# Later sums for the convolution's norm in a two-layer hybrid block on one Trainium2 core

## The chip, the cores and the metric

The kernel runs on one core of one Trainium2 chip, alone. The metric is the device time of one execution in microseconds: 1804.47 us, the median of three executions from 1803.35 to 1806.31 us. All arithmetic on the matrix engine (PE) takes float32 data that the kernel has split into a high and a low part, so each weight block is multiplied three times (high by high, high by low, low by high).

## The reference, cut to what matters

The model has two layers. In each, a normalised input `h` is projected and goes through three branches (sparse attention, retention, convolution). Each branch's output is projected to 1024 channels, multiplied by a sigmoid gate of its own, and the three are summed; then come an output projection and a feed-forward part.

```python
h = _rmsnorm(x, norm_mix[l]); z = h @ w_in[l]
...
y = lax.conv_general_dilated(u, kern, ...)        # 31 taps for each of 512 channels
y = _layernorm(y + dw_b, ln_g, ln_b)              # over the 512 channels of a token
o_conv = jax.nn.silu(y)
br = jnp.stack([o_nsa, o_ret, o_conv], axis=2)
proj = jnp.einsum('bsnc,ncd->bsnd', br, w_branch[l])
gate = jax.nn.sigmoid(m_g).reshape(B, S, N_BRANCH, D_MODEL)
merged = jnp.sum(gate * proj, axis=2)
x = x + merged @ w_out[l]
```

The norm of the convolution is the part that moves. It needs two sums over channels for each token (for the mean, and for the variance of what is left), and the second needs the first.

## The kernel before

**Layout.** Activations lie with channels on the 128 partitions and the 512 tokens along the row, so a sum over channels is made on PE: `column_sums` multiplies four blocks of 128 tokens by a column of ones, and `rows_to_bcast` spreads a value per token over all partitions by four transposes.

**Convolution.** 124 taps (31 for each of four blocks of channels) are multiply-add instructions on the vector engine (DVE, line 338). They are dropped one or two at a time behind other DVE work. What is left when attention starts, `late_taps`, is spread over the attention's 64 inner steps: a tap's place is found from the step's number over `T_SLOTS` (52), so the last tap stands behind step 51 of 0 to 63.

**Attention** runs as 16 units, numbered u = 4j + k here: j is one of four pairs of heads, k counts two groups by two kinds of attention. A unit makes scores (PE, from line 707 on, tile `sc`), adds a bias and finds the row's extreme (DVE, line 712), takes the exponential (ScalarE, ACT, line 714), scales (line 719), transposes (PE, line 722), splits the result (ACT line 727, DVE line 728), and multiplies it with the values (PE, tile `av`). Line 739 ends a pair's group with `on`. The score tile `S` has three buffers and `sc` two banks.

**Fillers.** The gates and the retention branch's products do not depend on attention. They stand in the list `pending`: 8 products `mix(1, RO, m)`, then 16 gates `gate_ahead` for the other two branches. A gate is 24 matmuls with 512 columns into one bank `mm`, then one DVE and one ACT instruction, and a store to DRAM. Its weight block is loaded by SP, copied by ACT (line 145) and split by GpSimd (POOL, line 148) ahead of it. One entry runs before attention; 19 are handed out after units 0 to 15 by `more` (one each, two after units 5, 10 and 15); the last four, `HELD`, come when attention has been traced. The PE instructions of the entries of unit u stand behind that unit's first score matmul (`issue_after(marks[u].ins)`).

**Banks.** All gates, products, `query` projections and also the norm's sums use the three PSUM banks of tag `mm`, which are given out in the order in which the program asks for them.

**Order.** A planner that simulates the kernel writes out a fixed order for each engine. It takes the ready instruction that comes first in the program; what the program asks for later may go first only while earlier work is not ready.

**The norm** is a generator, `conv_norm` (line 585), of four steps: three additions on DVE (588 to 590); mean sums on PE, spread, four subtractions (597), squares, additions (601); the sums of squares and the root (POOL, line 206); and last `rows_to_bcast`, then for each of four blocks a multiplication (608), a scaling (609), a tanh (611), a product (612), a copy and a subtraction (112, 113), which give the convolution's output `OC`. From unit 12 on, when no tap is left, `more` takes one step per unit, ahead of that unit's fillers: additions at unit 12, mean at 13, squares at 14, the last step at 15.

**After attention** come the splits of its output into `OS`, eight products `mix(0, OS, m)` (12 matmuls each), eight `mix(2, OC, m)` and the output projection. A mix loads its stored gate `g`, and DVE joins it with the product (464) and adds it to `merged` (468).

Of the kernel before, what the change touches and what calls it, by code (L numbers as in the profile page):

```python
# [66 lines left out]
def block_kernel(ctx: ExitStack, tc: tile.TileContext, a, out):  # L67
# [7 lines left out]

    T_ROT, T_SCORE, T_KEYS, T_SLOTS = 1, 2, 3, 52


    AHEAD, F_KEYS, HELD = 16, 1, 4

    def tl(pool, tag, bufs, shape=(P, T), dtype=F):
        count[0] += 1
        return pool.tile(list(shape), dtype, name=f"{tag}_{count[0]}", tag=tag, bufs=bufs)
# [7 lines left out]
    def small(shape, dtype=F):  # L93
        if math.prod(shape[1:]) <= 8:
            return tl(base, "n", 40, shape, dtype)
        return tl(base, "m", 7, shape, dtype)
# [3 lines left out]
    def ps(tag, shape=(P, T)):  # L100
        return tl(psum, tag, PS_BUFS[tag], shape)
# [51 lines left out]
    def wblock(src, nk=KC, n=P):  # L153

        return wsplit(raw(lambda t: [(t, src)], nk, n), nk, n)

    def proj(o, w, x, nk=KC):

        h, l = w
        for k in range(nk):  # L160
            xh, xl = x[k]
            mm(o, h[:, k, :], xh, k == 0, False)
            mm(o, h[:, k, :], xl, False, False)
            last = mm(o, l[:, k, :], xh, False, k == nk - 1)
        return last
# [104 lines left out]
    for l in range(DEPTH):  # L270
# [56 lines left out]
        todo = [(c, k) for c in range(4) for k in range(CW)]  # L327

        def conv_taps(n):

            while n and todo and todo[0][0] < len(us):
                c, k = todo.pop(0)
                n -= 1
                w, x = ccol[:, c, l * CW + k:l * CW + k + 1], us[c][:, k:k + T]
                if k == 0:
                    nc.vector.tensor_scalar(yc[c], x, w, par(20 + c), op0=OP.mult, op1=OP.add)
                else:
                    nc.vector.scalar_tensor_tensor(yc[c], x, w, yc[c], op0=OP.mult, op1=OP.add)  # L338
# [49 lines left out]
        for h in range(4):  # L388
            if h % 2 == 0:
# [3 lines left out]
                for i in range(NB):  # L393
# [3 lines left out]
                    m = small((P, 2))  # L397
# [17 lines left out]
            for j in range(NB):  # L415
                n = T - j * P
# [27 lines left out]
        def gate(n, m):  # L444
            pg = ps("mm")
            proj(pg, wblock(w_f[FB_MG + n * KC + m]), X)
            t = tl(base, "g", 3)
            nc.vector.tensor_mul(t, pg, rs)
            nc.scalar.activation(t, t, AF.Tanh, scale=0.5)
            return t  # L450
# [5 lines left out]
        def mix(n, o, m):  # L456
            if (n, m) in gated:
                t = tl(base, "g", 3)
                dma(t, gdram[n * KC + m])
            else:  # L460
                t = gate(n, m)
            po = ps("mm")
            proj(po, wblock(a["w_b"][l, n, m], 4), o, 4)
            nc.vector.scalar_tensor_tensor(t, t, 1.0, po, op0=OP.add, op1=OP.mult)
            if n == 1:
                dma(mdram[m], t)
            else:
                nc.vector.tensor_add(merged[m], merged[m], t)

        pending = [lambda m=m: mix(1, RO, m) for m in range(KC)]  # L470
# [3 lines left out]
        def fill(n):  # L474
            for _ in range(min(n, len(pending))):
                pending.pop(0)()
# [108 lines left out]
        def conv_norm():  # L585

            s, s2 = ut(), ut()
            nc.vector.tensor_add(s, yc[0], yc[1])
            nc.vector.tensor_add(s2, yc[2], yc[3])
            nc.vector.tensor_add(s, s, s2)  # L590
            yield
            mean = small((P, NB))
            nc.vector.tensor_scalar(mean, column_sums(s, tag="mm"), 1.0 / 512, None, op0=OP.mult)
            pm = rows_to_bcast(mean, "mm")
            acc = None
            for c in range(4):
                nc.vector.tensor_sub(yc[c], yc[c], pm)
                s = ut()
                nc.scalar.activation(s, yc[c], AF.Square)
                if acc is not None:  # L600
                    nc.vector.tensor_add(s, s, acc)
                acc = s
            yield
            rstd = rsqrt_rows(column_sums(acc, tag="mm"), 1.0 / 512)
            yield
            pr = rows_to_bcast(rstd, "mm")
            for c in range(4):
                nc.vector.tensor_mul(yc[c], yc[c], pr)
                nc.vector.tensor_scalar(yc[c], yc[c], par(24 + c), par(28 + c), op0=OP.mult, op1=OP.add)
                y = ut()  # L610
                nc.scalar.activation(y, yc[c], AF.Tanh, scale=0.5)
                nc.vector.scalar_tensor_tensor(y, y, 1.0, yc[c], op0=OP.add, op1=OP.mult)
                h, lo = tl(cp, "yc", 4, dtype=FR), ut(FR) if c < 3 else tmp(dtype=FR)
                split(h, lo, y)
                OC.append((h, lo))

        normed = conv_norm()
# [25 lines left out]
        def query(j):  # L643
            w = wblock(w_f[FB_Q + j])
            pq = ps("mm")
            proj(pq, w, X)
            tq = tl(ap, "tq", 2)
            nc.vector.scalar_tensor_tensor(tq, pq, -0.125, rs, op0=OP.mult, op1=OP.mult)
            return tq

        def attention_pair(j, tq, more):
            QS, bias = [], []
            for g in range(2):
# [41 lines left out]
            for g in range(2):  # L695
# [4 lines left out]
                for br in range(2):  # L700
# [30 lines left out]
                    for k, c0 in enumerate((0, 512, 896, 1152)):  # L731
                        n = T - k * P
                        lhs = V[k][:, 2 * br + g, :]
                        mm(av[:, k * P:], lhs, ph[:, c0:c0 + n], False, False)
                        mm(av[:, k * P:], lhs, pl[:, c0:c0 + n], False, br == 1 and k == NB - 1)
                    more(j, 2 * g + br)
                t = tmp()
                nc.scalar.activation(t[nat], av[oth], AF.Copy)
# [3 lines left out]
        ON, marks, tqs = [], [], [query(0)]  # L742
        late_taps = len(todo)

        def more(j, k):

            if k == 0 and j + 1 < HPG:
                tqs.append(query(j + 1))
            if not todo:
                next(normed, None)  # L750
            u = 4 * j + k
            with tc.issue_after(marks[u].ins):
                fill(paced * (u + 1) // 16 - paced * u // 16)

        for j in range(HPG):
            ON.append(attention_pair(j, tqs[j], more))
        conv_taps(len(todo))
        for _ in normed:
            pass
        with tc.issue_after(marks[-1].ins):  # L760
            fill(len(pending))

        phase.close()
        phase = ExitStack()
# [6 lines left out]
        for m in range(KC):  # L771
            merged[m] = tl(pp, "mg", 8)
            dma(merged[m], mdram[m])
            mix(0, OS, m)
        for m in range(KC):
            mix(2, OC, m)

# [110 lines left out]
```

## Time and profile before

| | |
|---|---|
| median of 3 executions | 1804.47 us |
| the profiled execution | 1804.74 us |
| its span | 1803.0 us |
| PE busy | 1757.3 us (97%) |
| DVE busy | 1104.4 us (61%) |
| ACT busy | 774.9 us (43%) |
| POOL busy | 500.6 us (28%) |

The times in the rows below count from the start of the span of this execution. A row of a timeline has start, duration, engine, line, operation, output and inputs, shape and count; what stands in brackets is the engine's idle time before it and what ended it. Matmuls overlap, so the distance of two starts is the price of what lies between, not the duration.

### The profile page before, as it was taken

How to read it: one execution, taken by the hardware profiler on the slowest of the kernel's cores; microseconds unless marked ns; L12 is line 12 of the kernel's file. 1: busy time of each engine (PE TensorE's matmuls, PEld its weight loads, DVE VectorE, ACT ScalarE, POOL GpSimd, SP SyncE). 2: the span in 40 equal slices, each digit the busy share in tenths (PEclk: the TensorE clock that was granted, in tenths of full speed). 3: DMA queues.
4: the chain of work that ended last, by engine and by line, in shares of the span. 5: the costliest groups of instructions: out<-in, count | busy, mean ns of one | idle time of the engine just before them, and what ended most of it. 6: DMA issues, size and time to landing. Idle time of an engine off the chain costs nothing.

```text
span 1803.0 us, 23260 instructions
## 1 busy us (share of the span) xinstructions
PE 1757.3 (97%) x8592; PEld 1473.8 (82%) x8592; DVE 1104.4 (61%) x1979; ACT 774.9 (43%) x1421; POOL 500.6 (28%) x420
## 2 busy tenths in 40 slices
PE   8899899989999999999999999999899999999997
PEld 7788788868888888888898888888688888888886
DVE  6976978887554344434459778878857443434344
ACT  4433466766343232323434344667553341323241
POOL 4454444323471000000255543343137500000000
PEclk9999999989999999999999999999899999999998
DMA  4222623221753323333422232332147323332321
GB/s 167 87 88 61 203 94 122 96 71 65 233 169 96 101 96 93 95 96 102 135 94 89 87 127 83 98 131 90 41 161 227 119 94 94 93 94 94 105 85 68
DMA packets 70802, 195.82 MB, mean 109 GB/s; under 512 B 8945, under 2 KB 9329, under 8 KB 70689
## 3 DMA queue, kind: packets, MB, share of 16 engines
q1 hardware_dynamic: 70688, 194.34, 33.6%
q8 instruction: 68, 1.11, 0.3%
q14 instruction: 46, 0.37, 0.1%
HBM read 177.51 MB, written 19.42 MB: 109 GB/s over the span
## 4 chain that ended last, share of the span: by engine, by line
PE 67%; issue 20%; DVE 10%; ACT 2%; DMA 1%; SPq 0%; POOLq 0%; POOL 0%; DVEq 0%; ACTq 0%
PE mm L109 58%; PE sc L109 3%; DVE yc L338 3%; PE av L109 3%; PE tp L722 2%; PE tp L109 1%; DVE XP L500 1%; DVE kv L563 1%; DVE qk L386 1%; ACT s L719 0%; DVE pt L728 0%; ACT wh L145 0%; DVE rr L364 0%; PE tp L190 0%; DVE s L712 0%
## 5 line engine op out<-in xcount | busy, mean ns | idle before, releaser
L109 PE MATMUL mm<-X,wh 128*128 128x512 f32 x2432 | 777.4, 396 | 12.2 <-ACT X L214 6.1
L148 POOL TENSOR_TENSOR wl<-wr,wh 128x512 fp32r<-128x512 f32 (+2 forms) x344 | 436.2, 1290 | 563.2 <-ACT wh L145 540.6
L145 ACT ACTIVATE wh<-wr 128x1024 fp32r<-128x1024 f32 (+2 forms) x301 | 296.9, 987 | 681.9 <-PE mm L109 554.5
L109 PEld LDWEIGHTS mm<-X,wh 128*128 128x128 f32 x2432 | 455.3, 189 | 103.1 <-ACT X L214 6.3
L109 PE MATMUL mm<-X,wl 128*128 128x512 f32 x1216 | 479.5, 394 | 0.4 <-DVE wl L150 0.4
L109 PEld LDWEIGHTS mm<-X,wl 128*128 128x128 f32 x1216 | 230.2, 189 | 46.5 <-DVE wl L150 0.9
L338 DVE SCALAR_TENSOR_TENSOR yc<-u,ccol,yc 128x512 f32<-128x512 f32 x240 | 214.2, 894 | 1.7
L150 DVE TENSOR_TENSOR wl<-wr,wh 128x1024 fp32r<-128x1024 f32 x129 | 158.1, 1225 | 38.4 <-ACT wh L145 38.4
L109 PE MATMUL mm<-fa,wh 128*128 128x512 f32 x512 | 160.2, 395 | 0.0
L109 PE MATMUL mm<-bo,wh 128*128 128x512 f32 x512 | 160.0, 391 | 0.0
L805 DVE SCALAR_TENSOR_TENSOR t<-mm,rs 128x512 f32<-128x512 f32 x64 | 43.9, 691 | 161.5 <-PE mm L109 155.9
L227 POOL TENSOR_TENSOR t<-t,t 128x512 f32<-128x512 f32 x18 | 27.4, 1523 | 333.7 <-DVE wl L150 310.7
L206 POOL TENSOR_TENSOR n<-n,mhalf 128x4 f32<-128x4 f32 x15 | 16.5, 1101 | 372.3 <-DVE n L204 372.3
L109 PE MATMUL mm<-kv,wh 128*128 128x512 f32 x384 | 119.5, 389 | 0.0
L109 PEld LDWEIGHTS mm<-fa,wh 128*128 128x128 f32 x512 | 96.1, 188 | 23.2
L109 PEld LDWEIGHTS mm<-bo,wh 128*128 128x128 f32 x512 | 96.0, 188 | 19.7
L109 PE MATMUL mm<-fa,wl 128*128 128x512 f32 x256 | 100.5, 395 | 0.0
L109 PE MATMUL mm<-bo,wl 128*128 128x512 f32 x256 | 100.2, 392 | 0.0
L714 ACT ACTIVATE s<-s,n 128x128 f32<-128x128 f32 (+3 forms) x128 | 71.4, 559 | 46.9 <-DVE n L712 46.3
L109 PE MATMUL mm<-wh,X 128*128 128x256 f32 (+1 forms) x480 | 90.1, 286 | 0.0
L728 DVE TENSOR_TENSOR pt<-tp,pt 128x128 fp32r<-128x128 f32 (+1 forms) x192 | 70.0, 372 | 32.7 <-ACT pt L727 32.4
L816 DVE TENSOR_TENSOR yc<-yc,mm 128x512 f32<-128x512 f32 x32 | 22.0, 687 | 105.6 <-PE mm L109 105.6
(219 smaller groups left out, 2463.9 us busy)
## 6 DMA issues: line engine op xcount, KB each, us to landing
wr<-in_w_dram SPq DMA_DIRECT2D x128, 512.0 KB, 3.5
wr<-in_w_f_dram SPq DMA_DIRECT2D x87, 512.0 KB, 3.3
wr<-in_w_b_dram SPq DMA_DIRECT2D x48, 256.0 KB, 2.7
wr<-in_w_t_dram SPq DMA_DIRECT2D x16, 512.0 KB, 3.4
gd<-g SPq DMA_DIRECT2D x32, 256.0 KB, 2.0
g<-gd SPq DMA_DIRECT2D x32, 256.0 KB, 2.8
wr<-in_w_o_dram SPq DMA_DIRECT2D x16, 512.0 KB, 3.6
md<-g SPq DMA_DIRECT2D x16, 256.0 KB, 2.9
```

The costliest lines, as they stand in the source:

```text
L109: return nc.tensor.matmul(o, l, r, start=start, stop=stop)
L145: nc.scalar.activation(h, t, AF.Copy)
L148: nc.gpsimd.tensor_sub(l[:, k], t[:, k], f(h[:, k]))
L150: nc.vector.tensor_sub(l, t, f(h))
L227: (nc.vector if c == KC - 1 or first_time else nc.gpsimd).tensor_add(s, s, acc)
L338: nc.vector.scalar_tensor_tensor(yc[c], x, w, yc[c], op0=OP.mult, op1=OP.add)
L386: nc.vector.tensor_sub(QLr[h][half], pt[nat], f(QHr[h][nat]))
L714: nc.scalar.activation(s, s, AF.Exp, scale=-1.0, bias=mx[:, i:i + 1], accum_out=den[:, i:i + 1])
L722: nc.tensor.transpose(pt[:, k * P:(k + 1) * P], cols[i][:, k * P:(k + 1) * P], ident)
L728: low = nc.vector.tensor_sub(vl, src, f(vh))
L805: nc.vector.scalar_tensor_tensor(t, pf, 0.0, rs, op0=OP.max, op1=OP.mult)
L816: nc.vector.tensor_add(xT[m], xT[m], pf)
```

## The change

The taps are spread over 56 steps in place of 52. No step of the norm is taken inside attention. When attention has been traced, the first step (additions) is taken and two held gates follow; the second step (mean, subtractions, squares), and the other two held gates; the third (sums of squares, root), and no gate. The last step comes in the loop of the first products, after `mix(0, OS, 1)`.

```diff
-    T_ROT, T_SCORE, T_KEYS, T_SLOTS = 1, 2, 3, 52
+    T_ROT, T_SCORE, T_KEYS, T_SLOTS = 1, 2, 3, 56
...
             if k == 0 and j + 1 < HPG:
                 tqs.append(query(j + 1))
-            if not todo:
-                next(normed, None)
             u = 4 * j + k
...
         conv_taps(len(todo))
-        for _ in normed:
-            pass
-        with tc.issue_after(marks[-1].ins):
-            fill(len(pending))
+
+        for n in (HELD // 2, HELD - HELD // 2, 0):
+            next(normed)
+            with tc.issue_after(marks[-1].ins):
+                fill(n)
...
             mix(0, OS, m)
+            if m == 1:
+                next(normed, None)
```

## Rows read from the trace of the kernel before

**Rows 1.** Page, part 2: PE busy and granted clock in 40 slices
```profile
PE   8899899989999999999999999999899999999997
PEclk9999999989999999999999999999899999999998
```

**Rows 2.** Windows: stretch, length, busy time and instructions by engine, PE clock, DMA
```profile
core 0: us, PE busy (x) PEld busy (x) DVE busy (x) ACT busy (x) POOL busy (x), PEclk, DMA share, GB/s
...
380.85:412.30 31.45, 24.43 (x112) 18.23 (x111) 27.36 (x78) 19.41 (x56) 2.64 (x2) 0.78 0.08 28
412.30:465.10 52.80, 52.80 (x261) 44.42 (x260) 32.50 (x67) 31.98 (x66) 17.37 (x15) 1.00 0.37 120
465.10:487.60 22.50, 22.50 (x98) 18.13 (x97) 13.23 (x15) 5.71 (x10) 13.72 (x16) 1.00 0.73 245
487.60:510.00 22.40, 22.40 (x99) 18.28 (x98) 17.54 (x22) 9.49 (x14) 16.43 (x15) 1.00 0.71 214
1264.45:1296.10 31.65, 24.90 (x111) 18.76 (x110) 27.29 (x75) 19.15 (x55) 2.63 (x2) 0.73 0.07 25
1296.10:1349.10 53.00, 53.00 (x261) 44.61 (x260) 32.51 (x67) 32.07 (x67) 17.38 (x15) 1.00 0.36 120
```

**Rows 3.** Timeline of PE in layer 0, around the end of attention
```profile
380.82 0.40 PE L109 MATMUL mm<-X,wl 128*128 128x512 f32 x1
...
386.13 0.44 PE L109 MATMUL sc<-kv,QS 128*128 128x128 f32 x2 [1.61 <-DVE n L712]
...
392.36 0.62 PE L109 MATMUL sc<-kv,QS 128*128 128x128 f32 x4
...
410.13 1.05 PE L109 MATMUL mm<-ones,u 128*128 128x1 f32 x8
...
412.31 0.71 PE L109 MATMUL mm<-X,wh 128*128 128x512 f32 x2
...
425.81 0.62 PE L109 MATMUL sc<-kv,QS 128*128 128x128 f32 x4
...
457.61 0.62 PE L109 MATMUL mm<-X,wh 128*128 128x512 f32 x2
...
465.09 0.62 PE L109 MATMUL mm<-os,wh 128*128 128x512 f32 x2
```

**Rows 4.** Timeline of DVE in layer 0, the same part
```profile
406.81 1.53 DVE L338 SCALAR_TENSOR_TENSOR yc<-u,ccol,yc 128x512 f32<-128x512 f32 x2
408.46 0.68 DVE L589 TENSOR_TENSOR u<-yc,yc 128x512 f32<-128x512 f32 x1
...
411.30 0.28 DVE L712 CUSTOM_DVE_ANT_0 s<-sc,bias 128x128 f32<-128x128 f32 x1
...
419.17 0.55 DVE L712 CUSTOM_DVE_ANT_0 s<-sc,bias 128x384 f32<-128x384 f32 x1
...
456.32 0.69 DVE L739 TENSOR_TENSOR on<-t,av 64x512 f32<-64x512 f32 x1 [2.51 <-ACT t L738]
```

**Rows 5.** Timeline of POOL: its first weight split after the stretch
```profile
419.52 1.28 POOL L148 TENSOR_TENSOR wl<-wr,wh 128x512 fp32r<-128x512 f32 x1 [34.67 <-ACT wh L145]
```

**Rows 6.** Groups on DVE by form, 425 to 448 us: the norm's last step
```profile
L612 DVE SCALAR_TENSOR_TENSOR u<-u,yc 128x512 f32<-128x512 f32 x4 | 3.1, 764 | 0.6 <-ACT u L611 0.6
...
L608 DVE TENSOR_TENSOR yc<-yc,mm 128x512 f32<-128x512 f32 x4 | 2.6, 679 | 0.0
L113 DVE TENSOR_TENSOR u<-u,yc 128x512 fp32r<-128x512 f32 x3 | 2.2, 729 | 1.3 <-ACT yc L112 1.3
...
L609 DVE TENSOR_SCALAR yc<-yc,pcol 128x512 f32<-128x512 f32 x4 | 1.9, 541 | 0.0
```

**Rows 7.** Timeline of DVE in the first mixing products
```profile
470.16 0.69 DVE L464 SCALAR_TENSOR_TENSOR g<-g,mm 128x512 f32<-128x512 f32 x1 [4.18 <-DMA g<-gd]
470.88 0.69 DVE L468 TENSOR_TENSOR mg<-mg,g 128x512 f32<-128x512 f32 x1
...
476.48 0.69 DVE L464 SCALAR_TENSOR_TENSOR g<-g,mm 128x512 f32<-128x512 f32 x1 [0.90 <-PE mm L109]
477.21 1.18 DVE L468 TENSOR_TENSOR mg<-mg,g 128x512 f32<-128x512 f32 x1
```

## The prediction

> **What bounds the kernel now.** I read the 40 slices first [rows 1]. PE is busy nearly everywhere at the full clock, so the kernel ends when PE has done its work, and time is to be had only where PE is idle or slow. Two slices in which both lines show an 8 (the ninth, and the twenty-ninth) lie at the end of the attention of layer 0 and of layer 1. Windows around them [rows 2] show the hole: from 380.85 to 412.30 us PE is marked busy 24.43 of 31.45 us and the clock granted is 0.78 of full, with 112 matmuls. Layer 1 has the same hole, 31.65 us long, at clock 0.73. Behind it, to 465.10 us, PE is full at clock 1.00, and so it stays through the mixing products.
>
> Why the hole is there, PE's timeline tells [rows 3]: the last gate matmul ends at about 381.2, the next one starts at 412.31, and what stands just before it is the norm's eight column-sum matmuls at 410.13 (and the spread of the mean). Nothing else kept the gate back. Its mark, the first score of unit 13, had run at 386.13, and its weights had been split since 384.85: POOL's next split, at 419.52, had waited 34.67 us [rows 5]. So the gate of unit 13 waited for its turn at the `mm` banks, behind sums that needed the last tap (line 338, 406.81) and the additions from 408.46 [rows 4]. The three banks stood empty, because the program asks for the norm's sums first.
>
> **How large the hole is.** A gate matmul costs 0.227 us: from 457.61 to 465.09 there are 33 of them, 11 rows of two and 11 of one [rows 3], 7.48 / 33. A gate of 24 is 5.44 us. From 412.30 to 465.10, eight gates (units 13, 14, two of 15, four held) take 192 matmuls, 43.5 us; the other 69 of the 261 take 9.3 us, 0.134 us each [rows 2]. At that price the 112 matmuls of the hole are 15.0 us of work at the full clock; its busy time times its clock (24.43 x 0.78 = 19.1) is the upper bound, since durations overlap. So the hole loses between 12.4 and 16.5 us. I take 16.5, as the price per matmul comes from the same kind of instructions at the full clock.
>
> **The change part by part.**
>
> *The norm's sums leave the turn inside attention.* After unit 12's gate the next askers are the gates of units 13 and 14, each held only by its mark, 386.13 and 392.36 [rows 3]. Both fit into the hole: 10.9 us of PE work. The norm's sums and spread, 12 matmuls (1.6 us), leave it. The pair of gates at unit 15 and the held four still need unit 15's first score. That one stood at 425.81, because unit 14's scores of 384 columns were read by DVE only at 419.17, and the two at 128 and 256 from 411.30 [rows 3, 4]; between lay the gates of units 13 and 14 and the norm's subtractions. With these gone, unit 15's score follows unit 14's DVE work at once. I put it at 413: DVE is busy 27.36 of 31.45 us in the hole [rows 2], so what sets the pace of units 12 and 13 stays: the same taps, two additions fewer that took 1.4 us (those at 408.46 and behind it), two gate instructions more (1.4 us). From 380.85 to 413, 32.15 us, PE then has 15.0 - 1.6 + 10.9 + some 1.3 us of attention that came just after 412.3, that is 25.6 us of work, and loses 6.5 us. The gain is 16.5 - 6.5 = 10 us a layer. Bounds: 5.4 us if only one gate fits, 16.5 if unit 15's score comes as early as units came with full PE, which closes the hole.
>
> *After 413* PE has six gates (32.6 us), attention's rest and the norm's sums, all ready, so it stays full, and mixing begins some 10 us earlier, at 455 in place of 465.09. Attention must be done by then. Before, the last `on` was made 31 us after unit 15's score (425.81 to 457.0) [rows 3, 4]; 413 + 31 is 444, and four splits end some 3 us later. Eight us of room, so I cost this at nothing; without that room each us late is a us of idle PE.
>
> *The norm's first three steps between the held gates.* The additions (2 us of DVE) come after the last tap, about 411, into a stretch in which DVE was busy 32.50 of 52.80 us [rows 2], and loses the last step there. They are wanted when PE has done four gates and 7 us of other work after 413, at 442. The mean's chain then has two held gates, 10.9 us, as cover for four subtractions, squares and additions. These took from 411.95 to about 417.2. Cost nothing. On POOL the root stands behind one weight split, 1.3 us [rows 5], covered too.
>
> *The last step among the products.* Its sixteen DVE instructions take 10.4 us by their rows [rows 6] (4 x 0.68, 4 x 0.54, 8 x 0.69 where nothing disturbs). Before, they lay beside gates, in a stretch with 20 us of free DVE. Now they stand between `mix(0, OS, 1)` and `mix(0, OS, 2)`, on an engine that is idle 9.3 us of the first 22.5, 4.2 of them in the wait before the first product is joined at 470.16, and 4.9 of the next 22.4 [rows 2, 7]. They are also slower there: the addition at line 468, two inputs in SBUF, takes 0.69 us when POOL is still and 1.18 beside POOL's splits, while line 464, with one input in PSUM, stays at 0.69 [rows 7]. With 0.49 us on eight instructions the step is 14.3 us. Free DVE from the first join to the end of the mixing is 5.1 + 4.9 = 10.0 us, so DVE ends up 0.4 to 4.3 us behind. The outputs are wanted one after the other from `mix(2, OC, 0)` on, some 15 us after the step can start, and DVE may put off its additions to `merged`; so I take 2 us a layer, with bounds of 0 (all put off into the output projection) and 4.3.
>
> The Trainium skill ("SBUF — State Buffer", section "Who interferes with whom") says that a DVE instruction with two SBUF inputs contends with a GpSimd instruction that reads SBUF, and one with a single SBUF input does not. The trace agrees: 1.18 against 0.69 us, and 0.69 unchanged. By that rule the eight two-input instructions of the step are the ones that stretch, and only while POOL, busy 13.72 of 22.5 us, is at work: 61% of 8 x 0.49 is an estimate of 2.4 us in place of 3.9.
>
> *Taps over 56 steps.* The same 124 instructions; the last move from unit 12 to unit 13 and still come before unit 14's DVE work. Nothing. No DMA is added; SP's stores of held gates and loads of mixing gates keep their order, and the first load of a mixing gate was already late (4.18 us of DVE's wait [rows 7]) without stopping PE, which has three banks.
>
> **Sum.** Per layer 10 - 2 = 8 us; layer 1's hole has the same length and counts; two layers 16 us, so the profiled execution's 1804.74 us (span 1803.0 and 1.7 around it) becomes 1788.7. The median stands 0.3 us lower: 1788.5, rounded to 1788.
>
> **Rivals.**
>
> *The hole closes wholly* and the last step hides: 2 x 16.5 = 33 us, 1771. For it: earlier units show no such hole, with the same gates [rows 1]. Against: DVE nearly full there, and unit 13's score came only at 386.13 after a wait on DVE, with no norm in its way. 0.12.
>
> *One gate only, or a dear last step.* If unit 14's gate comes after unit 15's score, the gain is 5.4 - 2 = 3.4 us a layer, 1798; with the last step at its 4.3 it is 1.1, 1802.5; the last step alone at that price gives 1793. For it: DVE's numbers in mixing. 0.17, of which 0.02 ends above 1801.
>
> *Slower: the held gates wait for the norm.* The additions now come after all attention in the program, and the third and fourth held gate behind the mean's sums in the turn. If DVE takes the additions only behind the last `on`, and that keeps its old end of 457, the sums run at 459; PE has finished its fourth gate at 442 and stands for 17 us, of which the hole's 10 were gained before; with the last step's 2 the layer is 9 slower, 1822 in all. It decides against the change once `on` ends after about 450 (wait over 8). Against it: attention has priority over these gates, and DVE has idle time for three additions. 0.06.
>
> *No effect*: the unit-13 gate waits for something else that I read as the turn. Then 1801 to 1808. 0.05.
>
> **How the numbers follow.** The forecast, 1781 to 1795, has 0.60. About 0.2% (3.6 us) is what a measurement of this kernel can tell from no change. Faster by more: 0.60 + 0.12 + 0.15 = 0.87; same 0.02 + 0.05 = 0.07; slower 0.06. The range, 1775 to 1800, leaves out half of the first rival, 0.02 of the second and the last two, 0.19 in all.
>
> **What would show it.** Right: gate matmuls on PE between 386 and 411, no `mm<-ones` before the held gates, the clock near 1.00 in the hole, unit 15's score by about 413, `mm<-os` at about 455, DVE full after the second product, and PE idle by 2 us at most before `mm<-yc`. Wrong: an idle PE ahead of the column sums (third rival), a hole as long as before (fourth), or PE waiting for line 113 in mixing for more than 5 us.

## The result, and the profile after

The changed kernel takes 1793.25 us, the median of five executions (1788.45 to 1796.39), against 1804.54 us for the kernel before in the same rounds: a ratio of 0.9935 with a 95% interval of 0.9917 to 0.9953. The profiled execution's span went from 1803.0 to 1791.5 us. The time lies in the predicted range, and 5 us above the predicted 1788. Direction and place were right; two terms of the sum were not.

The page of after, part 2, PE busy and granted clock in 40 slices; the two 8s of [rows 1] are gone from both lines:

```profile
PE   8899899999999999999999999999999999999997
PEclk9999999999999999999999999999999999999999
```

Windows of after in layer 0 (columns as in [rows 2]), and in a second view the same stretches of layer 1:

```profile
380.85:412.30 31.45, 29.16 (x153) 23.67 (x152) 23.32 (x73) 22.11 (x59) 8.47 (x6) 1.00 0.28 96
412.30:434.26 21.96, 21.96 (x109) 18.23 (x108) 13.59 (x32) 13.11 (x30) 8.54 (x6) 1.00 0.16 60
434.26:445.33 11.07, 9.36 (x43) 7.70 (x42) 6.92 (x16) 4.38 (x12) 1.86 (x2) 0.69 0.27 73
445.33:459.30 13.97, 13.97 (x74) 11.79 (x72) 8.89 (x17) 7.44 (x15) 1.53 (x3) 1.00 0.32 108
459.30:481.80 22.50, 22.50 (x100) 18.22 (x100) 19.51 (x31) 9.04 (x16) 17.71 (x16) 1.00 0.78 272
```
```profile
1264.45:1296.10 31.65, 29.93 (x154) 24.40 (x153) 21.01 (x59) 20.78 (x52) 8.40 (x6) 1.00 0.23 77
1312.50:1323.00 10.50, 8.79 (x40) 7.22 (x39) 6.46 (x16) 3.57 (x10) 1.79 (x2) 0.67 0.24 76
```

The old hole carries 153 matmuls in place of 112, at clock 1.00 in place of 0.78; PE is marked idle for 2.3 us of it. Behind it stands a hole that the kernel before did not have: 11.07 us with 43 matmuls, clock 0.69. Layer 1 has it too.

PE of after, layer 0, around the end of attention:

```profile
385.69 0.44 PE L109 MATMUL sc<-kv,QS 128*128 128x128 f32 x2 [0.57 <-DVE n L712]
385.96 0.67 PE L109 MATMUL mm<-X,wh 128*128 128x512 f32 x2
...
395.44 0.67 PE L109 MATMUL mm<-X,wh 128*128 128x512 f32 x2
...
406.86 0.33 PE L109 MATMUL sc<-kv,QS 128*128 128x128 f32 x2
...
418.01 0.60 PE L722 MATMUL tp<-ident,s 128*128 128x128 f32 x4
...
438.05 0.49 PE L109 MATMUL av<-pct,vc 128*128 128x512 f32 x1 [0.98 <-DVE on L739]
...
440.45 1.70 PE L109 MATMUL mm<-ones,u 128*128 128x1 f32 x8
...
445.33 0.73 PE L109 MATMUL mm<-X,wh 128*128 128x512 f32 x2
...
458.48 0.95 PE L109 MATMUL mm<-ones,u 128*128 128x1 f32 x8
459.30 0.71 PE L109 MATMUL mm<-os,wh 128*128 128x512 f32 x2
```

The gates of units 13 and 14 start at 385.96 and 395.44, right behind their marks, where before none ran until 412.31 [rows 3]. Unit 15's first score comes at 406.86 (before 425.81). The two gates of unit 15 and the first two held ones have run by 434.26, but the third held gate starts only at 445.33, behind the column sums of 440.45 and the mean's spread. Mixing starts at 459.30, 5.8 us before its old 465.09; in layer 1 it starts 12.2 us before (1336.72 and 1348.92), 7.2 of them new if layer 0's 5.0 (below) are taken off.

DVE of after, the same part:

```profile
419.10 0.29 DVE L712 CUSTOM_DVE_ANT_0 s<-sc,bias 128x128 f32<-128x128 f32 x1
...
436.39 1.01 DVE L338 SCALAR_TENSOR_TENSOR yc<-u,ccol,yc 128x512 f32<-128x512 f32 x1
437.33 0.67 DVE L739 TENSOR_TENSOR on<-t,av 64x512 f32<-64x512 f32 x1
438.26 0.67 DVE L589 TENSOR_TENSOR u<-yc,yc 128x512 f32<-128x512 f32 x1
...
457.18 0.69 DVE L739 TENSOR_TENSOR on<-t,av 64x512 f32<-64x512 f32 x1 [4.02 <-ACT t L738]
```

The last tap moved from 406.81 to 436.39 [rows 4], the additions follow it, and the last `on` stands at 457.18, where it stood before (456.32). So two things in after end together just ahead of mixing: PE's gates, put off by the sums' wait for the taps, and the attention.

The mixing itself hardly changed: from its first product to the next stage's first activation (line 214) it is 54.0 us before (465.09 to 519.1) and 54.8 after (459.30 to 514.1); in layer 1 54.0 and 55.1. The spread's four matmuls are now within it (from 464.96 to the next start at 465.43, 0.5 us).

### The profile page after: what moved, and what is told of

Read it like the earlier page. It is cut to its first block, busy times and chain, and to the rows that moved or that the text cites. A ratio compares the mean times of both kernels' runs of the same rounds, so it can differ in the third digit from the quotient of the medians.

```text
span 1791.5 us, 23230 instructions
## 1 busy us (share of the span) xinstructions
PE 1750.2 (98%) x8592; PEld 1469.7 (82%) x8592; DVE 1101.9 (62%) x1979; ACT 775.0 (43%) x1421; POOL 504.8 (28%) x420
## 4 chain that ended last, share of the span: by engine, by line
PE 68%; issue 20%; DVE 10%; ACT 1%; DMA 1%; SPq 0%; POOL 0%; POOLq 0%; DVEq 0%; ACTq 0%
PE mm L109 59%; PE sc L109 3%; PE av L109 3%; DVE yc L338 3%; PE tp L722 2%; PE tp L109 1%; DVE qk L386 1%; DVE XP L500 0%; DVE pc L684 0%; DVE rr L364 0%; DVE QS L657 0%; DVE s L712 0%; DVE pt L728 0%; DVE g L448 0%; DVE kv L563 0%
## 5 line engine op out<-in xcount | busy, mean ns | idle before, releaser
L728 DVE TENSOR_TENSOR pt<-tp,pt 128x256 fp32r<-128x256 f32 (+1 forms) x192 | 71.2, 375 | 65.0 <-ACT pt L727 64.3
L727 ACT ACTIVATE pt<-tp 128x256 fp32r<-128x256 f32 (+1 forms) x192 | 63.7, 340 | 58.6 <-PE tp L722 42.6
```

The source lines that it names most:

```text
L727: nc.scalar.activation(vh, src, AF.Copy)
L728: low = nc.vector.tensor_sub(vl, src, f(vh))
```

## The experiments

Twelve kernels ran, each with five to twelve executions beside the kernel before (1804.4 to 1804.8 us). A time is the median of a kernel's executions, a ratio is to the kernel before, with its 95% interval. Times of mixing below are of layer 0. Three theories were asked about: T, that the sums' wait for the late taps is what is lost; A, that the end of attention sets mixing's start; C, that the freed gates slow attention by their place in the written order.

**Taps over 52 steps.** The changed kernel with its old number of steps.

```diff
-    T_ROT, T_SCORE, T_KEYS, T_SLOTS = 1, 2, 3, 56
+    T_ROT, T_SCORE, T_KEYS, T_SLOTS = 1, 2, 3, 52
```

> The change with the taps over 52 steps again. In the trace of the changed kernel PE has finished the second held gate at 434.3 us and takes the next one at 445.3, after the mean's sums, which waited for the last tap (436.4); that stretch does 42 matmuls, some 5.6 us of work, in 11.1 us. Theory T (the turn at the banks, held by late taps): the last tap moves back from unit 13 to unit 12, some 10 us earlier, the sums are ready when PE wants them, and up to 5.5 us a layer come back: 1783 to 1788. Rival A (attention's end sets the start of mixing: its last output is made at 457.2 in both kernels and mixing starts at 459.3): PE only waits elsewhere, 1791 to 1795.

1797.08 us, ratio 0.9951 (0.9940 to 0.9963). Windows, then PE, then ACT, of this kernel:

```profile
380.85:412.30 31.45, 27.40 (x128) 22.36 (x127) 22.63 (x61) 21.03 (x55) 8.11 (x6) 0.89 0.23 76
...
434.00:446.00 12.00, 12.00 (x69) 10.22 (x67) 8.75 (x18) 7.42 (x17) 2.09 (x3) 1.00 0.22 69
446.00:459.30 13.30, 11.03 (x61) 8.77 (x60) 4.85 (x13) 6.01 (x16) 3.84 (x5) 1.00 0.55 185
```
```profile
436.49 0.95 PE L109 MATMUL mm<-ones,u 128*128 128x1 f32 x8
...
459.44 0.73 PE L109 MATMUL mm<-os,wh 128*128 128x512 f32 x2 [1.33 <-ACT os L112]
```
```profile
458.76 2.19 ACT L112 ACTIVATE os<-on 128x512 fp32r<-128x512 f32 x4
```

The second hole is gone (69 matmuls, clock 1.00), and nothing is won: the time lies above both ranges. PE now stands 2.3 us between 446 and 459.30, until the attention's output is split, and the first hole is larger, 128 matmuls in place of 153. Mixing starts at 459.44. T as a sufficient cause falls; A's wait is borne out, its time is not.

**The kernel before with taps over 56 steps.** The change's first line alone.

```diff
-    T_ROT, T_SCORE, T_KEYS, T_SLOTS = 1, 2, 3, 52
+    T_ROT, T_SCORE, T_KEYS, T_SLOTS = 1, 2, 3, 56
```

> The kernel before with only the taps over 56 steps. Its norm's steps follow one unit later, so the gate of unit 13 comes ahead of them in the turn and fills 5.4 us of the hole, while the last taps come later. Theory T: the hole moves and the mean's sums still hold the gates behind them; between 5 us a layer faster and 5 slower, 1795 to 1815. If it takes the whole gain of the change (1793 or less), the steps between the held gates earn nothing.

1809.89 us, ratio 1.0015 (1.0005 to 1.0026). One window and one line of PE:

```profile
404.00:425.00 21.00, 17.49 (x72) 13.82 (x73) 17.02 (x39) 9.98 (x29) 0.00 (x0) 0.67 0.01 1
```
```profile
419.49 1.05 PE L109 MATMUL mm<-ones,u 128*128 128x1 f32 x8
```

Its twelve executions lie between 1802.26 and 1810.15 us, with a mean of 1807.8, and the rows are of one that took 1803.70. The hole only moves with the taps: 72 matmuls in 21 us, and the next gate at 422.91 behind the sums of 419.49. So the taps alone gain nothing, and the norm's new place alone, which is the kernel with 52 steps above, takes 1804.51 to 1797.08. Whether 56 steps add to that is not shown: the two intervals, 0.9940 to 0.9963 and 0.9917 to 0.9953, overlap.

**The mean without the taps.** The first additions read two outputs of the attention in place of the convolution's, so the mean is of other data.

```diff
-            nc.vector.tensor_add(s, yc[0], yc[1])
-            nc.vector.tensor_add(s2, yc[2], yc[3])
+            nc.vector.tensor_add(s, ON[0], ON[1])
+            nc.vector.tensor_add(s2, ON[0], ON[1])
```

> The change with 56 steps, but the norm's first additions read two outputs of attention that are made long before in place of the convolution's blocks, so the sums for the mean do not wait for a tap (the mean is of the wrong data; the subtractions still wait for the taps). Theory T: the held gates follow at once, the stretch from 434 to 445 is full of gate matmuls, up to 5.5 us a layer, 1783 to 1788. Rival A: 1791 to 1795.

1791.77 us, ratio 0.9925 (0.9912 to 0.9937). PE of this kernel:

```profile
433.74 0.95 PE L109 MATMUL mm<-ones,u 128*128 128x1 f32 x8
...
457.78 0.73 PE L109 MATMUL mm<-os,wh 128*128 128x512 f32 x2 [1.33 <-ACT os L112]
```

With all of the taps' wait taken from the sums, they run at 433.74, and mixing starts 1.5 us earlier than in after, stopped by the same splits. That is all the second hole is worth while attention ends at 457.1; the time is in A's range.

**Taps over 44 steps.** As the first edit, with 44.

```diff
-    T_ROT, T_SCORE, T_KEYS, T_SLOTS = 1, 2, 3, 56
+    T_ROT, T_SCORE, T_KEYS, T_SLOTS = 1, 2, 3, 44
```

> The change with the taps over 44 steps: they end with unit 10. Theory T: sums surely ready in time, but 60 taps over 44 steps in place of 56 add about 0.3 taps (0.2 us of DVE) a step to units that are near full on DVE already; 1783 to 1790, not better than 52 steps by more than 3 us. Rival A: 1791 to 1796.

1791.38 us, ratio 0.9928 (0.9916 to 0.9940). The additions are done by 402, the sums still run only at 435.26, right behind the fourth gate in the turn, without a hole; mixing starts at 457.64, again with `[1.33 <-ACT os L112]`, the last `on` at 456.96. Same reading as the run before, in a kernel that leaves nothing out. The vector engine had little to do in it while attention ended, 8.65 us of 21.70 where after has 13.59 of 21.96, and PE was full:

```profile
412.30:434.00 21.70, 21.70 (x111) 18.24 (x110) 8.65 (x26) 12.61 (x30) 7.62 (x6) 1.00 0.19 60
```

**Without the last output.** 52 steps, and the split of the fourth pair's output reads the third's: the fourth is left out.

```diff
-            split(h, lo, ON[j])
+            split(h, lo, ON[min(j, 2)])
```

> The 52-step variant (1797.1 us), but the split of attention's last output reads the third pair's output, ready long before, in place of the fourth's (the fourth output is left out of the result). Rival A (attention's end sets the start of mixing): in the 52-step variant PE stands from about 455 to 459.4 for the splits; here it goes on at once, so 3 to 5 us a layer less: 1787 to 1791. Theory T (the banks' turn alone): no change, 1794 to 1798.

1796.29 us, ratio 0.9951 (0.9939 to 0.9964), as with 52 steps alone. ACT of this kernel:

```profile
460.36 2.19 ACT L112 ACTIVATE os<-on 128x512 fp32r<-128x512 f32 x4
```

All four copies of the splits still start with the last `on` (460.37), which none of them needs. So it is not, or not only, the data that they wait for.

**More held gates.** Six; eight; and eight with the taps over 44 steps (the line of the edit above).

```diff
-    AHEAD, F_KEYS, HELD = 16, 1, 4
+    AHEAD, F_KEYS, HELD = 16, 1, 6
```

> The change with six gates held in place of four (17 instead of 19 handed out during attention; three held ahead of the mean's sums and three behind). Rival A: with two gates fewer among the units attention ends earlier, and the two gates fill PE behind it; the last output by some 5 to 10 us earlier, 1785 to 1790. Theory T: one gate more stands ahead of the mean's sums and covers 5.4 us of the wait for the last tap, so 1785 to 1790 as well, but with the last output where it was (457). The trace tells them apart, not the time. If gates are not what delays attention, 1791 to 1796.

> The same with eight gates held (15 handed out, four ahead of the mean's sums, four behind). Rival A: attention ends 10 to 20 us earlier than 457, PE may idle a little among the last units, 1780 to 1788; better than six held. Theory T: no better than six held.

> Eight gates held and the taps over 44 steps, so that neither the sums nor attention's end should be late. Both limits gone: mixing starts when PE has done its work, 1778 to 1786, a little faster than eight held with 56 steps if the taps still hold the sums there, the same if not.

1798.06 us (ratio 0.9967, 0.9954 to 0.9980), 1811.21 (1.0037, 1.0025 to 1.0049) and 1810.07 (1.0034, 1.0022 to 1.0046). Fewer gates inside attention did not end it earlier: the last `on` came at 461.4 with six, at 462.0 with eight and at 460.2 with eight and 44 steps, and with eight PE was idle early in attention, where the gates were missing (14.26 us busy from 220 to 240 us, at clock 0.74). These expectations missed.

**Splits into memory of their own.** 52 steps; two pairs' outputs are split into buffers that do not take over the attention's memory, and used twice; the outputs of the other two pairs and their splits are left out.

```diff
-        for j in range(HPG):
-            h, lo = tl(pp, "os", 8, dtype=FR), tl(pp, "os", 8, dtype=FR)
+        for j in range(2):
+            h, lo = tl(a2, "os", 4, dtype=FR), tl(a2, "os", 4, dtype=FR)
...
+        OS = OS * 2
```

> As e1_slots52 (taps over 52 steps), but the splits of the attention's output are made of the first two pairs only, into buffers of their own that do not take over the attention's memory, and are used twice: the outputs of the third and fourth pair are left out of the projection, and two of four splits fall away. Theory A: once the sums come without a hole, mixing starts late only because these splits stand behind the end of attention (its last output, and the memory that it gives back); then the first mixing product moves from 459.4 us to about 454, when the gates are done, PE has no idle stretch from 450 to 460, and two layers save 7 to 11 us of e1's 1797: 1786 to 1790. Rival B: mixing waits for something else behind the gates (a loaded weight, a bank, DVE's work): start stays at 458 to 460 and the time at 1794 to 1798.

1801.08 us, ratio 0.9976 (0.9967 to 0.9986). PE, DVE and SP of this kernel:

```profile
449.07 0.71 PE L109 MATMUL mm<-os,wh 128*128 128x512 f32 x2
...
478.01 1.22 PE L109 MATMUL mm<-os,wh 128*128 128x512 f32 x2 [8.01 <-DVE g L464]
```
```profile
470.60 0.69 DVE L739 TENSOR_TENSOR on<-t,av 64x512 f32<-64x512 f32 x1
472.06 1.08 DVE L468 TENSOR_TENSOR mg<-mg,g 128x512 f32<-128x512 f32 x1 [0.77 <-DMA mg<-md]
```
```profile
469.04 2.80 SPq L773 DMA_DIRECT2D mg<-md  x6
473.17 0.32 SPq L459 DMA_DIRECT2D g<-gd  x1
```

What SP waited for in it, from 440 to 485 us (total, times, longest):

```profile
SPq L459 <- DVE mg L468: 8.3, 5, 2.6
```

Half of A is shown: with the splits' data and memory out of the way mixing starts at 449.07, 10.4 us earlier than with 52 steps alone. The time is above both ranges. The products now go ahead of attention, whose last `on` slips to 470.60, and another wait takes over. The loads of `mg` are issued only from 469.04, right behind attention's last products (from 468.58). `mg` too lies in the memory that attention gives back; that this holds them is likely but not shown, as SP's own order has them behind a weight load of 468.66. The first addition (468) waits for them until 472.06. The fourth gate load (473.17) waits for that addition, since `g` has three buffers, and PE stops for 8.01 us until that gate is joined with its product.

**Two of four splits in memory of their own.** On the kernel with 44 steps; nothing left out.

```diff
-            h, lo = tl(pp, "os", 8, dtype=FR), tl(pp, "os", 8, dtype=FR)
+            p = a2 if j < 2 else pp
+            h, lo = tl(p, "os", 4, dtype=FR), tl(p, "os", 4, dtype=FR)
```

> As e4_slots44 (taps over 44 steps), with the split outputs of the first two pairs in buffers of their own, the other two as before; nothing is left out. Theory A: the first half of each of the first three mixing products (18 matmuls, 4.1 us at 0.227) can be done while the last output is still awaited, so PE's idle 2 to 3 us between 450 and 460 are filled: 2 to 4 us a layer less than e4's 1791.4, 1784 to 1788. Rival B: all four splits are still written behind the end of attention, or the products wait for all four: 1790 to 1793, the first product at 457 to 459 as in e4.

1798.67 us, ratio 0.9969 (0.9958 to 0.9980): missed. PE, then DVE:

```profile
454.36 0.71 PE L109 MATMUL mm<-os,wh 128*128 128x512 f32 x2
...
461.25 0.70 PE L109 MATMUL mm<-os,wh 128*128 128x512 f32 x2 [0.91 <-DVE yc L608]
```
```profile
414.94 0.69 DVE L739 TENSOR_TENSOR on<-t,av 64x512 f32<-64x512 f32 x1 [4.17 <-ACT t L738]
...
463.90 0.69 DVE L739 TENSOR_TENSOR on<-t,av 64x512 f32<-64x512 f32 x1
```

Products begin at 454.36, but the last `on` moves from 456.96 to 463.90, and the splits of the other half come later by as much. The half products now stand on PE among attention's last steps; that they are what delays it is read, not tried (at the `on` before, 439.75 against 438.27 with 44 steps alone, attention was already 1.5 us late).

The kernel also settles why the copies wait, which the one without the last output left open. ACT, the copies of the second and the third pair:

```profile
360.92 0.62 ACT L112 ACTIVATE os<-on 128x512 fp32r<-128x512 f32 x1
...
463.83 0.63 ACT L112 ACTIVATE os<-on 128x512 fp32r<-128x512 f32 x1
```

The second pair's output was there at 359.45 + 0.69, and its copy, into memory of its own, follows at once. The third pair's was there at 414.94 + 0.69, and its copy, into memory that attention gives back, comes 48 us later, with the last `on`. The pool is all that the edit changed between them, so it is the memory that holds the copies.

**The gates one unit later in the program.** Marks unchanged: each unit's gates are asked for after the next unit.

```diff
-            u = 4 * j + k
-            with tc.issue_after(marks[u].ins):
-                fill(paced * (u + 1) // 16 - paced * u // 16)
+            u = 4 * j + k - 1
+            if u >= 0:
+                with tc.issue_after(marks[u].ins):
+                    fill(paced * (u + 1) // 16 - paced * u // 16)
...
+        with tc.issue_after(marks[-1].ins):
+            fill(paced - paced * 15 // 16)
```

> The changed kernel with one edit: the gates handed out after unit u come in the program after unit u+1 (their marks, so their earliest start, stay the same), so the attention of unit u+1 stands ahead of them in the program. Theory C: attention's units 12 to 14 got slower because the freed gates go ahead of the next unit in the written order (the last output stays at 457 though its first score came 19 us earlier); then the last output comes at 447 to 452, the last tap before 430, the second hole of 5 us goes, and the time is 1784 to 1789. Rival: units 12 to 14 are slow because of the vector engine's own work (taps and bias steps), wherever the gates stand: last output at 455 to 459, 1791 to 1796. If the gates come so late that PE idles between units 12 and 14 again, 1797 to 1803.

1791.32 us, ratio 0.9921 (0.9909 to 0.9933). PE, then DVE:

```profile
441.13 0.95 PE L109 MATMUL mm<-ones,u 128*128 128x1 f32 x8
...
456.85 0.71 PE L109 MATMUL mm<-os,wh 128*128 128x512 f32 x2
```
```profile
437.55 0.74 DVE L338 SCALAR_TENSOR_TENSOR yc<-u,ccol,yc 128x512 f32<-128x512 f32 x1
...
454.96 0.69 DVE L739 TENSOR_TENSOR on<-t,av 64x512 f32<-64x512 f32 x1 [4.45 <-ACT t L738]
```

The last `on` comes 2.2 us earlier, not the 5 to 10 that C asked; the last tap stays at 437.55, so the second hole stays too. Time and last `on` are those of the rival, but its cause, DVE's own work, is not borne out: with taps over 44 steps DVE was idle for 13 of 21.70 us, and the last `on` came at 456.96 all the same.

**Both: gates later and taps over 44 steps.** The last run, to see whether the two add: the edit above, and

```diff
-    T_ROT, T_SCORE, T_KEYS, T_SLOTS = 1, 2, 3, 56
+    T_ROT, T_SCORE, T_KEYS, T_SLOTS = 1, 2, 3, 44
```

> The changed kernel with two edits that the runs so far point to: the gates after a unit come one unit later in the program (as in f2_gates_one_unit_later, 1791.3 us, where attention's last output came at 455.0 but the last tap at 437.6 still left a hole), and the taps are spread over 44 steps (as in e4_slots44, 1791.4 us, where the sums came without a hole but the last output at 457.0). If the two limits of mixing's start are independent, as theory A has it (the sums' wait for the taps, and the end of attention), both go at once: last output at 452 to 455, no hole at the sums, mixing from 454 to 456, and 1 to 3 us a layer less than either: 1786 to 1790. Rival: the earlier taps go in where the vector engine holds up units 12 to 14, the last output goes back to 457 or later and the time is 1791 to 1796.

1791.98 us, ratio 0.9931 (0.9917 to 0.9945). The sums come without a hole (437.05), the last `on` at 458.74, mixing at 459.42. They do not add; C falls, and the rival's time and last `on` come again, without its cause.

The best three kernels that leave nothing out (1791.3 to 1792.0) have intervals that overlap that of the change (0.9917 to 0.9953). None can be told from it.

## Why the prediction was right, and where it was not

*The hole and its cause: right.* The gates of units 13 and 14 had waited for their turn at the banks behind the norm's sums and nothing else: taken out of the turn, they start at 385.96 and 395.44, and the clock in the stretch is 1.00. The kernel with the old norm and 56 steps confirms it from the other side. The hole closes better than forecast. Of the 153 matmuls now in it 72 are of gates; at the prediction's prices that is 16.3 + 10.9 = 27.2 us of work in 31.45, a loss of 4.2 where the step said 6.5. Unit 15's first score came at 406.86 rather than 413, and its gates with it.

*"After 413 PE has six gates, attention's rest and the norm's sums, all ready, so it stays full": wrong.* This is the failed term. The additions were put at about 411 on the ground that taps over 56 steps change nothing. The step numbers were right, their times were not: with two gates between them the units run later, and the last tap moved to 436.39. The sums at 440.45 hold the third gate until 445.33; in those 11.07 us PE did 43 matmuls, at the prediction's 0.134 us each 5.8 us of work, so 5.3 are lost. That is the third rival's mechanism (held gates behind the mean) with a smaller price and another cause: the tap, not DVE's order.

*"413 + 31 is 444; eight us of room": wrong, by 13 us.* The last `on` came at 457.18. The 31 us are no constant of attention: before, units 12 and 13 had their `on` at 417.75, ahead of unit 15's first score; in after that score came early and their `on` not until 437.33. PE now had the gates of units 13 and 14 among their steps, but that this is the reason is not shown: with the gates asked for one unit later that `on` came at 438.21. From unit 15's first score to the last `on` it was 50.3 us in after. What held unit 15 can be read but was not tried: its first scores stood from 406.86, DVE read them at 419.10, just behind unit 12's last transposes (418.01 + 0.60). Line 702 gives `S` three buffers, so unit 15 takes unit 12's. Then the units' products pass one after the other through the single bank `av`: unit 14's first, at 438.05, waited for the `on` of 437.33. In every kernel here that starts its products behind attention, the last `on` lies between 455.0 and 462.0, however taps, held gates and order were set; before it was 456.3. Why it lands there each time stays open; DVE's load it is not (44 steps, above).

*Which of the two counted.* Either alone holds mixing near 458: without the sums' wait it starts at 457.64 to 459.44, behind attention; and in after PE is full from 445.33 to 459.30, so its gates end there whatever attention does. The two errors cost the same microseconds, and easing one moved mixing's start by 2.5 us at most (456.85, gates one unit later). No kernel here was rid of both, so what they cost together is not measured.

*The last step among the products, 2 us: too dear.* Mixing took 0.8 us longer, 0.5 of it the spread's matmuls, which before lay ahead of it; 1.1 in layer 1. PE never stopped in it, so DVE, which did fill up (19.51 us of 22.5 after 13.23 [rows 2]), put off nothing that PE had to wait for. Groups on DVE by form, 464 to 489 us of after, with mean ns:

```profile
L468 DVE TENSOR_TENSOR mg<-mg,g 128x512 f32<-128x512 f32 x8 | 6.4, 814 | 0.1
...
L612 DVE SCALAR_TENSOR_TENSOR u<-u,yc 128x512 f32<-128x512 f32 x4 | 3.3, 816 | 0.0
L609 DVE TENSOR_SCALAR yc<-yc,pcol 128x512 f32<-128x512 f32 x4 | 2.7, 746 | 0.0
```

The step had been priced at 0.49 us more on each of eight instructions; the means are 0.82 us for line 612 (before 0.76 [rows 6]) and 0.81 for 468, since three quarters of either ran at 0.68 and the rest at about 1.22; of the step's eight two-input instructions that are slowed, only two were. Line 609 took 0.75 in place of 0.54, which was not in the sum. The whole step is 11.8 us of DVE against 14.3 priced.

*The sum.* Per layer, predicted 10 - 2; found in layer 0: a start of mixing 5.8 earlier, less 0.8 in it, 5.0 (the activations of line 214 at 514.1 and 519.1); in layer 1 a further 6.1; together 11.1 of the span's 11.5. Of the 16.5 us of the old hole 4.2 stayed lost and 5.3 went into the new one; 1.5 more were gone when unit 12 began (376.52 against 375.02), which no run explains (over the kernels with four held gates it lies between 374.0 and 377.5, without a pattern). That leaves 5.5 for the 5.8 found. So the total came as near as it did partly by luck: the better closed hole (2.3 us) and the cheaper last step (1.2) made up for half of what the new hole and the late start took (6.8).

## What to carry to other kernels

When a step is taken out of a turn that starved an engine, ask what it waits for where it is put: its inputs' times are set by work that the filled hole delays, so a time read before the change (the last tap, the 31 us of a unit) may not be carried over. Before a wait is removed, look for the chain that ends next to it; here the attention's last output (457.18) came 2 us ahead of mixing (459.30), and four later edits to the sums and gates bought nothing that could be measured. Memory handed from one phase to the next is a wait like any other: here it held a copy for 48 us after its data was there. And a step that is let go early can hold up what it overtakes.

## What the runs showed of the hardware

The contention between DVE and POOL went both ways. From 472.18 to 480.70 us DVE's instructions with two inputs in SBUF took 0.68 us though POOL was at work, and POOL's splits paid. DVE of after, then POOL, eight splits of 256 columns:

```profile
476.38 0.68 DVE L612 SCALAR_TENSOR_TENSOR u<-u,yc 128x512 f32<-128x512 f32 x1
...
480.70 1.22 DVE L468 TENSOR_TENSOR mg<-mg,g 128x512 f32<-128x512 f32 x1
```
```profile
474.72 10.79 POOL L148 TENSOR_TENSOR wl<-wr,wh 128x256 fp32r<-128x256 f32 x8 [0.66 <-ACT wh L145]
```

That is 1.35 us each, with single ones of up to 2.44, where the same split had a median of 0.74 (and at most 1.27) in before's mixing. From 480.70 on it is DVE again that stretches, to 1.22, though it ran one instruction behind the other there as before. The Trainium skill ("SBUF — State Buffer", section "Who interferes with whom") says that the order of issue decides which of the two is blocked; the trace agrees that either can be, at 2.44 against 0.74 us on POOL and 1.22 against 0.68 on DVE. What decides it was not tried. The same section excepts the engine's two-port modes, which `tensor_scalar` can enter, from its rule that one SBUF input does not contend; the prediction's telling leaves that out. Line 609, a `tensor_scalar` that reads one block from SBUF, took 0.96 us twice beside POOL's splits and 0.53 twice from 471.3 on, when POOL had paused (0.54 in the kernel before); whether it ran in such a mode no run shows.
